# A unit's decay weights, issued four steps later in a hybrid SSD layer in fp32

## The chip, the cores and the metric

One core of one Trainium2 chip. The metric is the device time of one execution in microseconds (us), the median of several runs. Before the change it is 1293.44 us (three runs, 1293.35 to 1298.07).

## The reference

One layer of a trunk: RMSNorm, a Mamba-2 mixer (SSD) with residual, and a final RMSNorm, for 512 tokens of width 2048 in fp32. Cut to what matters here:

```python
proj = rmsnorm(x) @ w_in                     # 512 x 2048 @ 2048 x 10304: z, x, B, C, dt
xs, B, C = split(silu(conv4(proj_xbc)))      # causal depthwise convolution of 4 taps
dt = softplus(dt + dt_bias);  a = -exp(a_log) * dt
# scan over chunks, 64 heads of 64 in 8 groups, state 128:
cs = cumsum(a);  decay[l, s] = exp(cs[l] - cs[s]) for l >= s, else 0
y = (C.B * decay) @ (xs * dt) + C @ state * exp(cs)
y = (y + d_skip * xs) * silu(z)
out = rmsnorm(x + rmsnorm(y) @ w_out)
```

## The kernel before

**Two halves of a number.** TensorE multiplies in a rounded 32-bit format (fp32r). Each weight piece of 128x1024 therefore is split (`split_piece`): ScalarE makes `hi`, the rounded copy (L87), and VectorE `lo`, the rest (L88). A product is then three matmuls for each slice of the inner dimension: activations' `hi` and `lo` with weight `hi` (L635, L636), activations' `hi` with weight `lo` (L637).

**Pairs and products.** The columns of `w_in` are worked off in tiles of 128. The first eight tiles are multiplied plainly. The other 72 go two by two, in 36 *pairs* (`pair`), each by a scheme of seven half-size products in place of eight (Strassen's way, on the two tiles, the two halves of the inner dimension and the two halves of the tokens). A pair has 28 *steps*, four to a product. In TensorE's order: R11, T1, then the last product T4 of the pair before (`prev`), T2, R22, R21 and T3. T3 is the seventh product issued within a pair, at steps 24 to 27; its weights come from a raw buffer named `rb`, which SP fills with one piece (L81) and a DMA of GpSimd's queue adds another to (L598, `accum_op`). There is one `rb`; the next load into it waits for its `lo`.

**Units.** A pair of an x tile and a z tile is a *unit* of two heads, numbered 0 to 31. Of each group of four units, a pair of a B tile and a C tile (a *B/C pair*) comes ahead of the third. After its pair a unit is worked on in five functions, at steps counted from the start of its own pair: `u_load` (28: SP loads `csb` and `ecs`), `u_decay`, `u_xt` (56), `u_state` (65), `u_yd` (65), `u_yo` (71).

`u_decay` makes the decay weights `m`: twelve activations on ScalarE of 128x128 (L456, L457, L458), which read `csb`, an exponential over 128x1024 (L459), and on VectorE the product with the masked C·B (L461). `m` and `csb` have one buffer each. `u_yd` on TensorE (L502, L506) reads `m`. `u_yd`, `u_yo` and the convolution (`conv_silu`: L388, L391) follow on VectorE; `u_yo` ends with a store by SP (L524), behind which the next loads of SP stand.

**What sets the order.** The program is written through a table `ev` of steps: `add(step, f, ...)` puts a function in, and `product` calls `run(step)` before every second slice. TensorE, SP and GpSimd issue in the order in which the program is written. For ScalarE and VectorE a scheduler sets the order at build time, by what it thinks is ready; what is written earlier goes first, and what stands under `urgent()` ahead of that. T3's split is written at step 17 (`q_events`: `(17, q_split, ("T3",))`), T1's of the next pair at 18, R11's of the pair after it at 19.

**Kinds of pairs**, by which unit's decay they hold (it belongs to the pair ahead). In a cycle of five: the *B/C pair* holds that of units 5, 9, 13, 17, 21 and 25; the *gap pair* right after it holds none; the *restart pair* after that holds that of units 6, 10, 14, 18, 22 and 26; two *ordinary pairs* hold those of 7 and 8, 11 and 12, and so on. Unit 2's is held by the second of all pairs, units 3 and 4 and 27 to 30 are in ordinary pairs. The two first units have a table of their own (`ramp`).

Of the kernel before, what the change touches and what calls it, by code (L numbers as in the profile page):

```python
# [34 lines left out]
def mamba_layer(ctx: ExitStack, tc: tile.TileContext, d: dict, out: bass.AP):  # L35
# [668 lines left out]
    def add(step, f, *a):  # L704
        ev.setdefault(step, []).append((f, a))
# [4 lines left out]
            add(at["x", 4 * g] + 28, g_cb, g, i)  # L710
    ramp = [[66, 71, 63, 75, 87, 92], [56, 65, 50, 68, 86, 92]]
    for u in range(NU):
        w = ramp[u] if u < len(ramp) else [28, 42, 56, 65, 65, 71]
        for o, f in zip(w, (u_load, u_decay, u_xt, u_state, u_yd, u_yo)):
            add(at["x", u] + o, f, u)
    for n in range(len(quads)):
# [395 lines left out]
```

## Time and profile before

| | |
|---|---|
| median of three runs | 1293.44 us |
| the profiled execution | 1295.7 us |
| its span, first to last instruction | 1294.0 us |
| mean granted TensorE clock | 0.991 |
| TensorE busy | 1252.1 us (97%) |
| VectorE busy | 1084.3 us (84%) |
| ScalarE busy | 826.6 us (64%) |
| DMA moved | 225.90 MB, mean 175 GB/s |

In the profile PE is TensorE's matmul, PEld its weight load, DVE VectorE, ACT ScalarE, POOL GpSimd, and SPq the queue of SyncE, which issues DMAs. A timeline row has the start and the duration in us, engine, line, operation, tiles written <- read, form and count, and in brackets the engine's idle time just before it with what ended it. A row of waits names who waited for whom, the sum in us, how often, and the longest. A row of time slices has, after the span, the busy time of PE, PEld, DVE, ACT and POOL with their instructions, then the granted clock, the DMA engines' busy share and GB/s. Ends of matmuls are modelled and overlap; so where the text counts matmuls it goes by starts.

### The profile page before, as it was taken

To read this page: it belongs to the slowest core of one execution; us is meant where nothing else is said; L and a number is where in the kernel's file an instruction comes from. 1 tells how busy PE (TensorE), PEld (TensorE's weight loads), DVE (VectorE), ACT (ScalarE), POOL (GpSimd) and SP (SyncE) were. 2 spreads that over 40 slices of the span, in tenths; PEclk is the share of its full clock that TensorE was granted. 3 is DMA by queue.
4 is the path that set the end of the run, shared out by engine and by line. 5 is a ranking of instruction groups with operands and counts; after the bars stand their busy time and mean duration, and the time that the engine had idled before them with its cause. 6 is when DMAs were issued, how large, how long until landed. Compare 5 with 4: busy or idle time off the path is not lost.

```text
span 1294.0 us, 24519 instructions
## 1 busy us (share of the span) xinstructions
PE 1252.1 (97%) x9932; PEld 1192.9 (92%) x9932; DVE 1084.3 (84%) x1449; ACT 826.6 (64%) x1357; POOL 77.5 (6%) x99
## 2 busy tenths in 40 slices
PE   8989899999999999999999999999999899999997
PEld 8989899999999999999999999999988899899885
DVE  5796988988989898998889899889857877887865
ACT  7667667677666757767685867778666445434433
POOL 0000001010000101010100001000000000000000
PEclk9989999999999999999999999999999999999999
DMA  9546657585676667667667677766637576647612
GB/s 356 179 141 172 162 161 174 143 215 142 192 197 174 159 169 183 164 176 199 162 161 195 151 188 171 212 155 154 185 105 258 146 199 199 197 119 229 183 57 98
DMA packets 70194, 225.90 MB, mean 175 GB/s; under 512 B 8384, under 2 KB 12800, under 8 KB 69952
## 3 DMA queue, kind: packets, MB, share of 16 engines
q1 hardware_dynamic: 56688, 176.34, 40.2%
q0 software_dynamic: 12672, 46.14, 22.1%
q8 instruction: 78, 1.28, 0.4%
q10 hardware_dynamic: 720, 1.84, 0.4%
q14 instruction: 36, 0.29, 0.1%
HBM read 211.52 MB, written 12.78 MB: 173 GB/s over the span
## 4 chain that ended last, share of the span: by engine, by line
PE 74%; DVE 11%; DMA 7%; issue 4%; ACT 3%; SPq 0%; POOL 0%; DVEq 0%; ACTq 0%; POOLq 0%
PE S L637 7%; PE S L635 7%; PE S L636 7%; PE mm L635 5%; PE mm L636 4%; PE R L635 4%; PE mm L637 4%; PE R L636 4%; PE R L637 4%; DVE lo L88 3%; PE mm L929 3%; PE mm L931 3%; PE mm L930 3%; PE yd L502 2%; PE mm L867 2%
## 5 line engine op out<-in xcount | busy, mean ns | idle before, releaser
L87 ACT CAST hi<-ra 128x1024 fp32r<-128x1024 f32 x150 | 154.7, 1046 | 159.5 <-DVE ra L604 72.9
L88 DVE TENSOR_TENSOR lo<-ra,hi 128x1024 fp32r<-128x1024 f32 x150 | 181.3, 1221 | 24.2 <-ACT hi L87 24.1
L635 PE MATMUL mm<-xh,hi 128*128 128x256 f32 x576 | 163.6, 284 | 0.0
L637 PE MATMUL mm<-xh,lo 128*128 128x256 f32 x576 | 160.6, 279 | 0.6 <-DVE lo L88 0.6
L636 PE MATMUL mm<-xl,hi 128*128 128x256 f32 x576 | 160.4, 278 | 0.0
L637 PE MATMUL R<-s,lo 128*128 128x256 f32 x576 | 160.3, 278 | 0.1
L635 PE MATMUL R<-s,hi 128*128 128x256 f32 x576 | 160.2, 278 | 0.0
L636 PE MATMUL R<-s,hi 128*128 128x256 f32 x576 | 160.2, 278 | 0.0
L88 DVE TENSOR_TENSOR lo<-rc,hi 128x1024 fp32r<-128x1024 f32 x94 | 114.9, 1223 | 28.5 <-ACT hi L87 28.1
L87 ACT CAST hi<-rc 128x1024 fp32r<-128x1024 f32 x94 | 98.4, 1047 | 50.8 <-issue 29.1
L604 DVE TENSOR_TENSOR ra<-ra,rc 128x1024 f32<-128x1024 f32 x88 | 107.7, 1224 | 13.3 <-DMA rc<-in_wi 11.8
L635 PEld LDWEIGHTS mm<-xh,hi 128*128 128x128 f32 x576 | 108.1, 188 | 5.2 <-issue 5.0
L637 PEld LDWEIGHTS mm<-xh,lo 128*128 128x128 f32 x576 | 109.2, 190 | 0.8 <-DVE lo L88 0.8
L637 PEld LDWEIGHTS R<-s,lo 128*128 128x128 f32 x576 | 109.1, 189 | 0.3 <-DVE lo L88 0.3
L635 PEld LDWEIGHTS R<-s,hi 128*128 128x128 f32 x576 | 108.2, 188 | 0.0
L636 PEld LDWEIGHTS mm<-xl,hi 128*128 128x128 f32 x576 | 108.2, 188 | 0.0
L636 PEld LDWEIGHTS R<-s,hi 128*128 128x128 f32 x576 | 108.1, 188 | 0.0
L637 PE MATMUL S<-xh,lo 128*128 128x256 f32 x288 | 83.5, 290 | 5.6 <-DVE lo L88 5.6
L635 PE MATMUL S<-xh,h1h 128*128 128x256 f32 x288 | 83.4, 290 | 1.0 <-DVE xr L398 1.0
L635 PE MATMUL S<-xh,hi 128*128 128x256 f32 x288 | 81.3, 282 | 2.2 <-ACT xh L577 1.3
L636 PE MATMUL S<-xl,hi 128*128 128x256 f32 x288 | 81.2, 282 | 0.7 <-DVE xl L578 0.7
L636 PE MATMUL S<-xl,h1h 128*128 128x256 f32 x288 | 80.8, 280 | 0.0
(452 smaller groups left out, 3940.8 us busy)
## 6 DMA issues: line engine op xcount, KB each, us to landing
rc<-in_wi SPq DMA_DIRECT2D x76, 512.0 KB, 5.9
ra<-in_wi SPq DMA_DIRECT2D x42, 512.0 KB, 6.2
rb<-in_wi SPq DMA_DIRECT2D x40, 512.0 KB, 6.9
ra<-in_wi POOLq DMA_DIRECT2D x36, 512.0 KB, 6.3
rb<-in_wi POOLq DMA_DIRECT2D x36, 512.0 KB, 5.9
csb<-cscr SPq DMA_DIRECT2D x32, 512.0 KB, 8.0
ra<-in_wo SPq DMA_DIRECT2D x26, 512.0 KB, 5.4
yscr<-xs SPq DMA_DIRECT2D x32, 256.0 KB, 2.6
```

The lines of the kernel that those rows point to most:

```text
L87: S.copy(out=hi, in_=raw)
L88: V.tensor_tensor(out=lo, in0=raw, in1=hi, op=ALU.subtract)
L502: T.matmul(pyd[r, i, :], x[:, 2 * i, hh, :], m[:, i, hh::4, :], start=i == 0, stop=False, skip_group_check=True)
L604: V.tensor_tensor(out=raw, in0=raw, in1=qs[n][other], op=ALU.add)
L635: T.matmul(ps, hi[:, k, :], ah, start=first and k == 0, stop=False, skip_group_check=True)
L636: T.matmul(ps, hi[:, k, :], al, start=False, stop=False, skip_group_check=True)
L637: T.matmul(ps, lo[:, k, :], ah, start=False, stop=k == KH - 1, skip_group_check=True)
L867: T.matmul(ps[:, t, :], yh[:, k, tt], hi[:, k, :], start=st, stop=False, skip_group_check=True)
L929: T.matmul(ps, yh, hi, start=first and k == 0, stop=False)
L930: T.matmul(ps, yh, lo, start=False, stop=False)
L931: T.matmul(ps, yl, hi, start=False, stop=last and k == 1)
```

## The change

The second number of the table of a unit's steps: `u_decay` is written at step 46 after its pair's start in place of 42, which is step 18 of the pair that holds it in place of 14. It then stands behind T3's split (17) and, at the same step, ahead of T1's.

```diff
     for u in range(NU):
-        w = ramp[u] if u < len(ramp) else [28, 42, 56, 65, 65, 71]
+        w = ramp[u] if u < len(ramp) else [28, 46, 56, 65, 65, 71]
         for o, f in zip(w, (u_load, u_decay, u_xt, u_state, u_yd, u_yo)):
             add(at["x", u] + o, f, u)
```

The same instructions are issued as before. The order on TensorE, SP and GpSimd is the same row by row; on SP the load of `csb` now has a wait for ScalarE of its own in most units. On ScalarE and VectorE the order changes from unit 2 on.

First, ScalarE in the pair that holds unit 2's decay, from the copy out of PSUM (L674) on. L87 is the cast of T3's weights, L394 the silu of a convolution. Before:

```order
L674 COPY sn<-S 128x256
L458 ACTIVATE m<-csb,nwl 128x128
L456 ACTIVATE m<-csb,cs 128x128
L457 ACTIVATE m<-csb,cs 128x128
L458 ACTIVATE m<-csb,nwl 128x128
L456 ACTIVATE m<-csb,cs 128x128
L457 ACTIVATE m<-csb,cs 128x128
L458 ACTIVATE m<-csb,nwl 128x128
L459 ACTIVATE m<-m 128x2x512
L394 ACT_TABLE_LOAD
L394 ACTIVATE xs<-xs 128x512
L87 CAST hi<-rb 128x1024
```

After:

```order
L674 COPY sn<-S 128x256
L87 CAST hi<-rb 128x1024
L458 ACTIVATE m<-csb,nwl 128x128
L456 ACTIVATE m<-csb,cs 128x128
L457 ACTIVATE m<-csb,cs 128x128
```

The cast moved ahead of the last seven activations, the exponential and the silu. VectorE in the same pair, before and then after (L391: convolution, L679: half of z):

```order
L88 TENSOR_TENSOR lo<-rc,hi 128x1024
L391 SCALAR_TENSOR_TENSOR xs<-xr,par,xs 128x512 x2
L679 TENSOR_TENSOR z<-R,sn 128x256
L461 TENSOR_TENSOR m<-m,cbm 128x1536
L88 TENSOR_TENSOR lo<-rb,hi 128x1024
L88 TENSOR_TENSOR lo<-ra,hi 128x1024 x2
```

```order
L88 TENSOR_TENSOR lo<-rc,hi 128x1024
L391 SCALAR_TENSOR_TENSOR xs<-xr,par,xs 128x512
L88 TENSOR_TENSOR lo<-rb,hi 128x1024
L679 TENSOR_TENSOR z<-R,sn 128x256
L391 SCALAR_TENSOR_TENSOR xs<-xr,par,xs 128x512
L461 TENSOR_TENSOR m<-m,cbm 128x1536
L88 TENSOR_TENSOR lo<-ra,hi 128x1024 x2
```

T3's `lo` moved ahead of L461, of L679 and of one convolution step. VectorE in an ordinary pair (unit 3's decay; the others alike, and in B/C pairs L679 and `lo` both go ahead of L461), before and after:

```order
L523 TENSOR_TENSOR xs<-xs,z 128x512
L461 TENSOR_TENSOR m<-m,cbm 128x1536
L88 TENSOR_TENSOR lo<-rb,hi 128x1024
L529 TENSOR_TENSOR sx<-sx,z 128x512
L679 TENSOR_TENSOR z<-R,sn 128x256
```

```order
L523 TENSOR_TENSOR xs<-xs,z 128x512
L88 TENSOR_TENSOR lo<-rb,hi 128x1024
L461 TENSOR_TENSOR m<-m,cbm 128x1536
L529 TENSOR_TENSOR sx<-sx,z 128x512
L679 TENSOR_TENSOR z<-R,sn 128x256
```

L461 and T3's `lo` changed places; on ScalarE the cast of `rb` moved there ahead of the copy L674, the last L457 and L458, and L459. In the restart pairs the rows are the same before and after, on VectorE these (and on ScalarE the cast of `rb` behind L459):

```order
L391 SCALAR_TENSOR_TENSOR xs<-xr,par,xs 128x512 x2
L461 TENSOR_TENSOR m<-m,cbm 128x1536
L391 SCALAR_TENSOR_TENSOR xs<-xr,par,xs 128x512
L679 TENSOR_TENSOR z<-R,sn 128x256
L88 TENSOR_TENSOR lo<-rb,hi 128x1024
```

Nothing moved there.

## The prediction

> **What bounds the kernel now.** I read the page's head first, then TensorE's list of waits over the stretch in which the 36 pairs run (100 to 960 us), then the timelines at its waits.
>
> ```profile
> span 1294.0 us, 24519 instructions
> PE 1252.1 (97%) x9932; PEld 1192.9 (92%) x9932; DVE 1084.3 (84%) x1449; ACT 826.6 (64%) x1357; POOL 77.5 (6%) x99
> PE S L637 <- DVE lo L88: 5.6, 9, 1.5
> ```
>
> TensorE is busy for 97%, so only its waits can be gained. The largest group among the pairs is `S L637 <- lo`: 5.6 us in nine places. All nine lie in the seventh product (T3), whose rounded weights `hi` and rest `lo` are made from the buffer `rb`. These are the rows of five of those pairs, and of one whose wait is too small for the list.
>
> ```profile
> 163.27 0.28 PE L637 MATMUL mm<-xh,lo 128*128 128x256 f32 x1
> 164.45 0.38 PE L635 MATMUL S<-xh,hi 128*128 128x256 f32 x1 [0.91 <-ACT hi L87]
> 165.71 0.58 PE L637 MATMUL S<-xh,lo 128*128 128x256 f32 x1 [0.76 <-DVE lo L88]
> 235.69 0.28 PE L636 MATMUL S<-xl,hi 128*128 128x256 f32 x1
> 236.13 0.39 PE L637 MATMUL S<-xh,lo 128*128 128x256 f32 x1 [0.17 <-DVE lo L88]
> 347.12 0.39 PE L637 MATMUL S<-xh,lo 128*128 128x256 f32 x1 [0.17 <-DVE lo L88]
> 390.02 0.38 PE L637 MATMUL S<-xh,lo 128*128 128x256 f32 x1 [0.47 <-DVE lo L88]
> 501.43 0.39 PE L637 MATMUL S<-xh,lo 128*128 128x256 f32 x1 [1.54 <-DVE lo L88]
> 412.39 0.38 PE L637 MATMUL S<-xh,lo 128*128 128x256 f32 x1
> 412.60 0.28 PE L635 MATMUL S<-xh,hi 128*128 128x256 f32 x1
> ```
>
> Matmuls normally start 0.11 to 0.12 us apart. A wait costs more than its idle time: 235.69 to 236.13 is 0.44, so 0.33 too long, and the start after the first `lo` matmul comes 0.10 late, as 412.39 to 412.60 shows. So the small waits (0.17) cost about 0.42 us each, and a pair whose `lo` comes just in time (412) costs 0.10.
>
> The pairs fall in kinds (named in the kernel section). Unit 2 waits at 164; restart pairs have the big waits (0.47 at 390, 1.54 at 501; of the 5.6 us they hold four, about 4.2); B/C pairs have 0.17 each (236 and 347 are two); ordinary pairs have the 0.10.
>
> **Unit 2, the pair at 164 us.** ScalarE casts T3's `hi` after the whole decay and a silu, and VectorE subtracts after the product with the masked C·B (L461).
>
> ```profile
> 158.14 0.37 ACT L674 COPY sn<-S 128x256 f32<-128x256 f32 x1
> 158.41 0.41 ACT L458 ACTIVATE m<-csb,nwl 128x128 f32<-128x128 f32 x1
> 163.37 1.03 ACT L87 CAST hi<-rb 128x1024 fp32r<-128x1024 f32 x1
> 159.60 1.53 DVE L391 SCALAR_TENSOR_TENSOR xs<-xr,par,xs 128x512 f32<-128x512 f32 x2
> 161.55 1.76 DVE L461 TENSOR_TENSOR m<-m,cbm 128x1536 f32<-128x1536 f32 x1
> 164.43 1.23 DVE L88 TENSOR_TENSOR lo<-rb,hi 128x1024 fp32r<-128x1024 f32 x1 [1.12 <-ACT hi L87]
> 141.70 0.88 POOL L598 DMA_DIRECT2D rb<-in_wi  x1 [9.09 <-DVE xr L576]
> rb<-in_wi POOLq DMA_DIRECT2D x36, 512.0 KB, 5.9
> 165.57 2.35 DVE L88 TENSOR_TENSOR lo<-ra,hi 128x1024 fp32r<-128x1024 f32 x2
> 177.03 0.65 PE L502 MATMUL yd<-m,xd 128*64 128x256 f32 x4
> 158.89:162.30 3.41, 3.41 (x33) 3.41 (x32) 3.29 (x5) 3.39 (x8) 0.00 (x0) 1.00 1.02 315
> 162.30:165.71 3.41, 1.74 (x13) 1.34 (x12) 2.29 (x3) 3.40 (x5) 0.00 (x0) 1.00 0.48 183
> 165.71:169.12 3.41, 3.41 (x16) 3.41 (x17) 3.35 (x3) 0.58 (x1) 0.00 (x0) 0.50 0.66 193
> ```
>
> In the new order the cast follows the copy at 158.14, so it can run 158.41 to 159.4; `rb` was asked for at 141.70 and at the median landing time of 5.9 us was there by 147.6. VectorE's first of the two convolution steps ends about 160.3, then `lo` takes 1.1 to 1.2 (from start to next start), until about 161.5. T3 could start at 163.27 + 0.11 = 163.4, so both waits go. What they cost: 1.18 + 1.04 us between starts where 0.11 each is normal, plus 0.4 in the two ramps after them, 2.4 us. The three slices at the end of the fence tell the rest; the third number from the right is TensorE's granted clock. After the slice with the waits (13 matmuls) it is 0.50 for one slice (16 matmuls); undisturbed, a slice holds 33. 29 matmuls are 29/33 x 3.41 = 3.0 us of work, done in 6.8: 3.8 us, of which I take 3.7. So the half clock is 1.3 of it. What is put behind has cover: ScalarE's decay ends 1.0 later, at 162.5, L461 follows until about 164.2, and the first reader of `m` stands at 177.03, some 9 us later when all moves up by 3.7. Next late would be the second product's `lo<-ra`, the first of the two that run from 165.57: it is ready at 166.8 as before, and TensorE would now want it at 163.4 + 2.7 (T3) + 0.4 (transposes) + 2.8 (first product) = 169.3.
>
> [...]
>
> **Ordinary and B/C pairs.**
>
> ```profile
> 407.77 1.05 ACT L459 ACTIVATE m<-m 128x1024 f32<-128x1024 f32 x1
> 408.73 1.04 ACT L87 CAST hi<-rb 128x1024 fp32r<-128x1024 f32 x1
> 409.44 1.75 DVE L461 TENSOR_TENSOR m<-m,cbm 128x1536 f32<-128x1536 f32 x1
> 411.11 1.22 DVE L88 TENSOR_TENSOR lo<-rb,hi 128x1024 fp32r<-128x1024 f32 x1
> 423.42 0.44 PE L502 MATMUL yd<-m,xd 128*64 128x256 f32 x2
> 338.27 0.69 DVE L398 TENSOR_TENSOR xr<-mm,rbc 128x512 f32<-128x512 f32 x1 [1.50 <-PE mm L637]
> 338.27:367.77 29.50, 29.33 (x257) 28.56 (x256) 29.46 (x42) 19.50 (x34) 1.73 (x2) 1.00 0.59 146
> ```
>
> The cast moves ahead of the last two decay steps and the exponential over all of `m`, some 1.8 us; `lo` and L461 change places, so `lo` ends at 410.7 where it ended at 412.3. L461 then starts at 410.6; its input, ready at 408.8, comes 1.0 later, 409.8, so nothing waits. It ends at 412.3, 11 us ahead of `yd` (423.42). SP's next load of `rb` waits for this `lo` (one buffer), so it and the csb load behind it go out about 1.7 us earlier; csb must now wait for the decay's last read, about 408.8, ahead of that. On POOL's queue the accumulate into `rb` comes earlier too. DMA is the same in kind and amount.
>
> The waits that stay won: unit 5's B/C pair (236), 0.42, since its restart pair has no wait now; the 0.10 of row 412.60, in ten ordinary pairs of units 7 to 30, 1.0. Together 1.4.
>
> The B/C pairs' waits are not won for good. From the convolution at 338.27, the last place where VectorE waited for TensorE, to `lo` at 367.77 it is busy for 29.46 of 29.50 us: its time is then set by its own work, which the swap leaves as it was. What hangs on its end is the restart pair:
>
> ```profile
> 368.63 0.62 SPq L440 DMA_DIRECT2D csb<-cscr  x1
> 377.53 0.40 ACT L456 ACTIVATE m<-csb,cs 128x128 f32<-128x128 f32 x1 [0.39 <-DMA csb<-cscr]
> 388.75 1.22 DVE L88 TENSOR_TENSOR lo<-rb,hi 128x1024 fp32r<-128x1024 f32 x1
> ```
>
> SP issues csb right after that `lo`, it lands 8.9 us later, ScalarE starts the decay at once, and T3's `lo` follows at 388.75. In the restart pairs the rows of VectorE and ScalarE stand in the old order (last extract of the change): L461 is still ahead of `lo`. A TensorE that is 0.42 earlier out of the B/C pair waits 0.42 longer here. So for units 9, 21, 25 (0.42) and 13, 17 (0.10) I count nothing, and nothing for the 4.2 us of the restart pairs.
>
> **Sum:** 3.7 + 1.4 = 5.1 us. The profiled execution took 1295.7, 1.7 outside its span of 1294.0; it becomes 1290.6. It lies 2.3 above the median of 1293.44, from which the forecast is 1288.3, 0.40% less. Runs of this kernel tell 0.5% (6.5 us) from no change, so this is within it.
>
> One thing is not in the sum: the matmul pace.
>
> ```profile
> 241.93:244.65 2.72, 2.72 (x27) 2.72 (x26) 2.72 (x5) 1.32 (x2) 0.84 (x1) 1.00 0.07 27
> 264.03:266.85 2.82, 2.82 (x26) 2.82 (x25) 2.79 (x3) 2.81 (x6) 0.86 (x1) 1.00 0.53 114
> ```
>
> These are two second products of 24 equal matmuls, no wait in either: 2.72 and 2.82 us. Which pace holds changes only where the stream is broken (a wait, the small matmuls of a unit), and every removed wait may change what follows. Over 36 x 7 = 252 products that is 25 us between all slow and all fast; some 70 independent stretches, split evenly, give about ±2 us (an estimate from these rows). It takes no side.
>
> **Rivals.**
> 1. More than 0.5% faster: the pace falls on the fast side by 2 us, or csb lands 0.5 us earlier in the five restart pairs because `rb` and csb of the pairs ahead are out of the way sooner (2.5 us). Either gives about 1286, both 1283.8. For it: csb took 8.9 us here, with four weight loads ahead of it. Against: those four stand as before.
> 2. Unit 2 gives less. (a) The half clock does not hang on these waits and stays: 1.3 less, 1289.6; against it, the slice of 0.50 follows the waits at once. [...] (b) Another wait takes the place at 164 us: up to 3.7 less, 1292.0; against it, the 2.5 us that `lo<-ra` has to spare.
> 3. The swap frees nothing: all waits reappear in the restart pairs, 1293.4. Against: between unit 2 and the next restart pair VectorE waits for TensorE at L398, as at 338.27, and so moves up with it.
> 4. Slower: the cast, now earlier in ScalarE's order, waits for `rb`, and everything behind it waits too.
>
> ```profile
> 333.36 0.87 POOL L598 DMA_DIRECT2D rb<-in_wi  x1 [20.59 <-DMA rb<-in_wi]
> 343.12 1.03 ACT L87 CAST hi<-rb 128x1024 fp32r<-128x1024 f32 x1
> ```
>
> At unit 9 it moves from 343.1 to 341.3 us; issued at 333.4, `rb` has 2 us to spare at 5.9. TensorE, which reads this `lo` from about 346.8, feels a landing only after 344.2, that is from 10.8 us on; at 11.1 us, 0.3 in each of some 24 pairs, it costs 7 us, 1300. The median is half of that.
>
> **Chances:** the forecast 0.52 (its own range 1286 to 1290.8, a quarter of it beyond 0.5%), rival 1 0.22, rival 2 0.17 (a 0.09, b 0.08), rival 3 0.05, rival 4 0.04. Range 1284.5 to 1292.5, which leaves out the slower case, no gain at all, and the far end of rival 1. Faster by over 0.5%: 0.22 + 0.13 = 0.35; slower 0.04; the rest 0.61.
>
> **What would show it.** No wait and no clock of 0.50 near 160 to 170 us; `lo<-rb` ahead of L461 by a clear margin, and no `S L637 <- lo` wait in ordinary and B/C pairs; four or five such waits left, all in restart pairs, the ones after B/C pairs longer by up to 0.4. If the restart pairs' waits vanish too, my chain from csb is wrong; if unit 2's time does not come back, rival 2.

## The result, and the profile after

| | before | after |
|---|---|---|
| median | 1293.35 us, 7 runs (1289.91 to 1298.07) | 1285.82 us, 7 runs (1283.94 to 1287.64) |
| profiled execution | 1295.7 us | 1284.84 us |
| its span | 1294.0 us | 1283.1 us |

The ratio is 0.9934, 95% interval 0.9916 to 0.9951: 0.66% less, 6 to 11 us. The forecast was 1288.3, so the gain is inside the range given and 2.5 us larger than forecast. The time is that of rival 1, by its pace half.

The head of the page after, and TensorE's largest wait among the pairs:

```profile
span 1283.1 us, 24537 instructions
PE 1242.2 (97%) x9932; PEld 1183.7 (92%) x9932; DVE 1084.2 (84%) x1449; ACT 829.1 (65%) x1357; POOL 77.7 (6%) x99
PE S L637 <- DVE lo L88: 7.5, 6, 1.8
```

The wait for T3's `lo` fell from nine places to six, but grew from 5.6 to 7.5 us: all six are restart pairs. TensorE's busy time fell by 9.9 us though it does the same matmuls (the 18 instructions more are waits for semaphores, 14 of them SP's ahead of `csb`). Most of that, 6.9 us by the count below, is the pace, the part that the forecast left at nothing.

**Unit 2.** TensorE's timeline at its T3, then ScalarE's and VectorE's around it, and two slices of 3.41 us from T3 on, with the clock, which was 0.50 behind this place before:

```profile
161.61 0.28 PE L637 MATMUL mm<-xh,lo 128*128 128x256 f32 x1
161.73 0.28 PE L635 MATMUL S<-xh,hi 128*128 128x256 f32 x1
161.96 0.28 PE L637 MATMUL S<-xh,lo 128*128 128x256 f32 x1
156.54 1.06 ACT L87 CAST hi<-rb 128x1024 fp32r<-128x1024 f32 x1
158.07 1.22 DVE L88 TENSOR_TENSOR lo<-rb,hi 128x1024 fp32r<-128x1024 f32 x1
160.65 1.76 DVE L461 TENSOR_TENSOR m<-m,cbm 128x1536 f32<-128x1536 f32 x1 [0.37 <-ACT m L459]
161.47:164.88 3.41, 3.41 (x31) 3.41 (x30) 2.28 (x3) 2.98 (x4) 0.73 (x1) 1.00 0.93 371
164.88:168.29 3.41, 3.41 (x32) 3.41 (x31) 3.41 (x6) 1.18 (x3) 0.13 (x1) 1.00 0.75 91
```

`lo` ends at 159.29, 2.4 us ahead of T3; no wait, and the clock stays at 1.00.

**Restart pairs.** The two whose waits were 0.47 (at 390) and 1.54 (at 501) before:

```profile
382.21 0.39 PE L637 MATMUL S<-xh,lo 128*128 128x256 f32 x1 [1.56 <-DVE lo L88]
493.66 0.39 PE L637 MATMUL S<-xh,lo 128*128 128x256 f32 x1 [1.83 <-DVE lo L88]
491.60:495.00 3.40, 1.57 (x14) 1.37 (x13) 3.37 (x5) 2.78 (x3) 0.00 (x0) 1.00 0.29 107
495.00:498.40 3.40, 3.40 (x18) 3.40 (x17) 2.56 (x3) 0.93 (x1) 0.37 (x1) 0.50 0.95 321
```

Both waits grew. After the slice that holds the second (14 matmuls) the clock is 0.50 for one slice: the half clock that went at 165 us came back at 495. Matmuls start 0.21 us apart in that slice in place of 0.11, which over its 3.40 us comes to about 1.6 us.

**An ordinary pair** (unit 7), TensorE around T3's first `lo` matmul, before and then after:

```profile
300.32 0.28 PE L637 MATMUL mm<-xh,lo 128*128 128x256 f32 x1
300.66 0.39 PE L637 MATMUL S<-xh,lo 128*128 128x256 f32 x1
300.88 0.28 PE L635 MATMUL S<-xh,hi 128*128 128x256 f32 x1
301.00 0.28 PE L636 MATMUL S<-xl,hi 128*128 128x256 f32 x1
297.71:300.43 2.72, 2.72 (x26) 2.72 (x25) 2.72 (x3) 2.69 (x5) 0.00 (x0) 1.00 0.63 193
307.93:310.75 2.82, 2.82 (x26) 2.82 (x25) 2.79 (x4) 1.64 (x3) 0.86 (x1) 1.00 0.36 80
```

```profile
293.45 0.28 PE L637 MATMUL mm<-xh,lo 128*128 128x256 f32 x1
293.79 0.28 PE L637 MATMUL S<-xh,lo 128*128 128x256 f32 x1
293.90 0.28 PE L635 MATMUL S<-xh,hi 128*128 128x256 f32 x1
290.84:293.56 2.72, 2.72 (x26) 2.72 (x25) 2.72 (x3) 2.69 (x4) 0.00 (x0) 1.00 0.65 182
300.76:303.48 2.72, 2.72 (x26) 2.72 (x25) 2.69 (x5) 1.85 (x3) 0.86 (x1) 1.00 0.30 100
```

Before, the start behind the first `lo` matmul comes 0.22 after it in place of 0.11. It cost 0.10 there, as the forecast had it. But the product ahead of this T3 took 2.72 us and the second product behind it 2.82: the small lateness was where the slow pace began. After, with `lo` 1.5 us ahead, the pace stays at 2.72.

Counted over the trace (starts of neighbouring matmuls of the pairs 112 to 114 ns apart are fast, 117 to 119 slow): 3018 fast and 2766 slow before, 4575 and 1222 after. The means are 113.34 and 117.78 ns. 1557 more starts at the shorter distance, by 4.44 ns each, are 6.9 us. *Fast share* below is the part that fast starts have in both kinds together.

**Where the 10.9 us between the two spans went**, read from the start of T3's first `lo` matmul in each unit's pair: 2.25 us lie ahead of unit 2 (a half clock at 77 us lasted two slices in one execution and one in the other, in code that the change leaves alone); 3.5 are unit 2's; 4.3 lie between units 3 and 30; 0.85 in the tail. The medians lie only 7.5 apart; the 2.25 and the 0.85, 3.1 in all, lie ahead of the first pair that the change touches and behind the last.

### The profile page after: what moved, and what is told of

The parts are those of the page before. It is cut to its first block, busy times and chain, and to the rows that moved or that the text cites. A ratio compares the mean times of both kernels' runs of the same rounds, so it can differ in the third digit from the quotient of the medians.

```text
span 1283.1 us, 24537 instructions
## 1 busy us (share of the span) xinstructions
PE 1242.2 (97%) x9932; PEld 1183.7 (92%) x9932; DVE 1084.2 (84%) x1449; ACT 829.1 (65%) x1357; POOL 77.7 (6%) x99
## 3 DMA queue, kind: packets, MB, share of 16 engines
q10 hardware_dynamic: 720, 1.84, 0.4%
## 4 chain that ended last, share of the span: by engine, by line
PE 72%; DVE 12%; DMA 8%; issue 4%; ACT 3%; SPq 0%; POOL 0%; DVEq 0%; ACTq 0%; POOLq 0%
PE S L637 6%; PE S L635 6%; PE S L636 6%; PE mm L635 4%; PE R L635 4%; PE R L637 4%; PE R L636 4%; PE mm L636 4%; PE mm L637 4%; DVE lo L88 3%; PE mm L929 3%; PE mm L931 3%; PE mm L930 3%; PE mm L867 3%; PE mm L868 3%
## 5 line engine op out<-in xcount | busy, mean ns | idle before, releaser
L87 ACT CAST hi<-ra 128x1024 fp32r<-128x1024 f32 x150 | 155.2, 1049 | 152.2 <-DVE ra L604 86.1
L88 DVE TENSOR_TENSOR lo<-rc,hi 128x1024 fp32r<-128x1024 f32 x94 | 114.9, 1222 | 23.6 <-ACT hi L87 23.3
L87 ACT CAST hi<-rc 128x1024 fp32r<-128x1024 f32 x94 | 98.7, 1050 | 44.7 <-issue 22.8
L604 DVE TENSOR_TENSOR ra<-ra,rc 128x1024 f32<-128x1024 f32 x88 | 107.7, 1224 | 13.3 <-DMA rc<-in_wi 11.9
```

The source lines that it names most:

```text
L87: S.copy(out=hi, in_=raw)
L88: V.tensor_tensor(out=lo, in0=raw, in1=hi, op=ALU.subtract)
L604: V.tensor_tensor(out=raw, in0=raw, in1=qs[n][other], op=ALU.add)
```

## The experiments

Theory W says that only waits and their ramps count, and that the pace falls by chance; theory P that a late `lo` at T3 starts a slow stretch. The kernel before was timed again with each set of runs (medians 1293.71, 1293.87 and 1294.92 us); a ratio is to the one of its own set.

**Only unit 2.**

```diff
- [28, 42, 56, 65, 65, 71]
+ [28, 46 if u == 2 else 42, 56, 65, 65, 71]
```

> Step 46 for unit 2 alone, 42 for all others. Both theories expect what the prediction counted for unit 2: 3.7 us off the kernel before (ratio 0.997), no slice at half clock near 165 us, T3's lo ready about 2 us early in that pair. The theory that only waits count (W) and the theory that T3's late lo also sets the matmul pace (P) agree here: the share of matmuls that start 112 to 114 ns apart stays near the 52% of before, since the other units keep the late lo.

Measured 1290.22 us, ratio 0.9970 (0.9954 to 0.9986): 3.9 us by the ratio, 3.5 by the medians, against 3.7 forecast. Fast share 54%. No slice of 0.50 lies near 165 us. Unit 2's term stands.

**All but unit 2** (`42 if u == 2 else 46`).

> Step 46 for every unit but 2. Theory W: 1.4 us off the kernel before (ratio 0.9989), the pace as it falls, near 52% fast. Theory P: a late lo, even by 0.1 us, breaks the stream and leaves the next stretch at the slow pace; with lo ready the fast pace holds through ordinary pairs, so the fast share is 75% or more, as in the changed kernel (79%), and 4 to 5 us go (ratio 0.996 to 0.997). Unit 2's waits and the half clock near 165 us stay under both.

Measured 1290.81 us, ratio 0.9978 (0.9963 to 0.9994), 2.8 us. Fast share 80%. The wait and the half clock at 165 us stay, and in one restart pair the clock drops as in the changed kernel (first two rows); behind a wait as long, at 499.57, it does not (next two):

```profile
383.60:387.00 3.40, 1.56 (x14) 1.37 (x13) 3.40 (x5) 3.37 (x4) 0.00 (x0) 0.99 0.56 213
387.00:390.40 3.40, 3.40 (x18) 3.40 (x17) 3.14 (x3) 0.39 (x1) 0.00 (x0) 0.50 0.73 231
496.20:499.61 3.41, 1.57 (x15) 1.37 (x13) 3.41 (x5) 3.38 (x5) 0.00 (x0) 1.00 0.58 205
499.61:503.00 3.39, 3.39 (x30) 3.39 (x31) 3.36 (x4) 1.34 (x2) 0.00 (x0) 1.00 0.64 203
PE S L637 <- DVE lo L88: 8.9, 7, 1.8
```

So the pace does go over to the fast side. The time alone does not decide: its interval holds both W's 0.9989 and P's 0.996 to 0.997. The restart pairs, which hold 8.2 of the 8.9 us, take part of the pace back.

**The split earlier instead of the decay later**: T3's split written at step 13, the decay left at 42.

```diff
- (17, q_split, ("T3",))
+ (13, q_split, ("T3",))
```

> The decay back at step 42, and in its place T3's split issued four steps earlier (13 in place of 17), so that it is ahead of the decay from the other side. In this order T3's lo goes ahead of L461 in the restart pairs too, and ScalarE has six table loads more per cycle or fewer. If the lateness of T3's lo is all that counts: at least what the changed kernel gained (7.5 us), and the restart pairs' waits (7.5 us in six) shrink below 2 us in all, together 1277 to 1283. If the decay's later place itself counts (csb's load, SP's queue, ScalarE's order): no better than the kernel before, 1290 to 1294, with new waits elsewhere.

Measured 1308.65 us, ratio 1.0115 (1.0091 to 1.0139): slower than either expectation. TensorE waits elsewhere, on ScalarE's copies (L684) and on the `lo` of other products; that the scheduler moved this work behind the earlier cast is an inference from its rule and was not followed row by row:

```profile
PE mm L635 <- ACT mm L684: 6.3, 5, 1.8
PE S L637 <- DVE lo L88: 4.7, 9, 1.2
PE R L637 <- DVE lo L88: 4.1, 5, 1.0
PE S L929 <- ACT hi L87: 3.3, 1, 3.3
```

It is another order and not the same change from the other side; on W and P its time says nothing.

**The ordinary pairs alone, and the B/C pairs alone**, each with unit 2.

```diff
+ [28, 46 if u == 2 or u % UPG in (0, 3) else 42, 56, 65, 65, 71]   # ordinary (not units 29 and 30)
+ [28, 46 if u == 2 or u % UPG == 1 else 42, 56, 65, 65, 71]        # B/C (and unit 29)
```

> Decay at step 46 for unit 2 and for the units in ordinary pairs (3, 4, 7, 8, 11, 12 and so on); at 42, as before, for the units in B/C and restart pairs. Theory P (a `lo` that is late at T3, by however little, puts TensorE back on the slow matmul pace for the products behind it): the ordinary pairs' share of the pace comes with it. Fast starts rise from 52% to about 68%, slow ones fall to about 1850, worth some 4 us beside the 3.7 of unit 2 and the 1.0 of the ordinary pairs' own lateness: 1285 to 1286.5. Theory W (only the waits count, and the pace falls by chance): 3.7 + 1.0, 1289.0, with a fast share that need not move. In both the restart pairs' waits stay near those of before (5 us in 8 places), since the B/C pairs are as before.

> The other half: decay at step 46 for unit 2 and for the units in B/C pairs (5, 9, 13, 17, 21, 25), at 42 for all others. Theory P: the B/C pair's late `lo` goes, so the products of the gap pair behind it run fast; fast share about 62%, 2 to 2.5 us beside the 3.7 of unit 2 and 0.4 of unit 5, given back in part by longer waits in the restart pairs (6 to 7.5 us in all): 1287.5 to 1288.5. Theory W: 3.7 + 0.4, and the B/C pairs' own 0.42 handed on to the restart pairs: 1289.5.

Measured: ordinary 1286.43 us, ratio 0.9927 (0.9903 to 0.9950), fast share 64%; B/C 1290.30 us, ratio 0.9963 (0.9946 to 0.9979), fast share 52%. The ordinary half gives what the change gives beside unit 2, 3.8 us by the medians where their own lateness is 1.0. That is outside W (1289.0, a ratio of 0.9962) and within P's 1285 to 1286.5. The B/C half adds nothing that shows to unit 2. Its interval holds both W's 1289.5 and P's 1287.5 to 1288.5, but the fast share that P forecast, about 62%, did not come. The gap pairs stayed slow although no T3 of a B/C pair has a late `lo` any more: in all six the slow stretch (240 to 249 starts) begins within T4, behind the small matmuls of a unit (L488, L502, L506). Two equal products of the gap pair at 350 us, ahead of these matmuls and behind them:

```profile
349.71:352.43 2.72, 2.72 (x26) 2.72 (x25) 2.72 (x6) 1.37 (x3) 0.86 (x1) 1.00 0.09 11
360.50:363.32 2.82, 2.82 (x26) 2.82 (x25) 2.82 (x7) 1.43 (x3) 0.00 (x0) 1.00 0.02 6
```

**`csb` earlier in the restart pairs** (16, 20 or 6 in place of 28, on the changed kernel). The edit takes in units 2 and 30 too, which also leave 2 on division by four.

```diff
- [28, 46, 56, 65, 65, 71]
+ [16 if u % UPG == 2 else 28, 46, 56, 65, 65, 71]   # 20 and 6 in the others
```

> The changed kernel, with the csb and ecs loads of the restart pairs' units written 12 steps earlier (16 in place of 28), ahead of the four weight loads in SP's order; VectorE still has L461 ahead of T3's lo there. Theory C (restart waits hang on csb's landing): csb lands about 4 us earlier in those pairs, the six waits of 1.2 to 2 us go or fall below 0.5, and 5 to 7 us go on top of the changed kernel, about 1279 to 1281. Theory V (they hang on VectorE's own work from the B/C pair on): the waits stay within 0.5 us of what they are and the time is the changed kernel's, 1285 to 1287.

> The changed kernel, with the loads of `csb` and `ecs` for the restart pairs' units at step 20 in place of 28. There the scheduler puts T3's `lo` ahead of the last convolution step and of L679 (some 1.0 to 1.1 us of VectorE), but still behind L461. Theory V (VectorE's own row of work sets when `lo` comes in a restart pair): `lo` comes 1.0 to 1.5 us earlier than in the changed kernel, the waits there fall from 7.5 to about 1 us, the half clock after 491 us goes: about 1279. Theory C (the landing of `csb` sets it, through the decay on ScalarE): with `csb` asked for earlier the waits go too; what tells the two apart is the room ahead of `lo` on VectorE. By V VectorE is busy without a break from the convolution to `lo`; by C it stands idle ahead of L461.

> The changed kernel, with those loads at step 6: the decay of the restart pairs' units then runs one pair earlier, in the gap pair, and L461 no longer stands ahead of T3's `lo` in the restart pair, which so comes some 2 us earlier there. V and C alike: no wait for `lo` in the restart pairs, 7.5 us less, with the half clock after 491 us gone some 8: 1278 to 1279. Against it: twelve more loads of an activation table on ScalarE in the gap pairs and L461 among VectorE's work there, which could make T3's or the next product's split late in the gap pair; each wait of 0.5 us there would cost 3 us over six pairs, 1281. Pace: with only the B/C pairs' stretch left slow, the fast share stays near 80% or rises.

Step 16: 1283.35 us, ratio 0.9913 (0.9887 to 0.9939); one of its six runs took 3897.62 us and is not in the ratio, the others took 1281.09 to 1284.54. Step 20: 1284.74, ratio 0.9919 (0.9897 to 0.9940). Step 6: 1275.67, ratio 0.9857 (0.9833 to 0.9881). The waits for T3's `lo`, in this order (with step 6 none is left):

```profile
PE S L637 <- DVE lo L88: 5.9, 6, 1.5
PE S L637 <- DVE lo L88: 3.0, 5, 0.7
```

With steps 16 and 20 neither theory's forecast came: the waits shrank from 7.5 us, but five of six stayed above the 0.5 us of C (step 16), and all together above V's 1 us (step 20), and the times lie outside C's 1279 to 1281 and V's 1285 to 1287 (step 16) and V's 1279 (step 20).

ScalarE and VectorE in one restart pair (unit 10), in the changed kernel and then with step 16:

```profile
364.15 1.23 DVE L604 TENSOR_TENSOR ra<-ra,rc 128x1024 f32<-128x1024 f32 x1 [2.05 <-DMA rc<-in_wi]
369.71 0.41 ACT L456 ACTIVATE m<-csb,cs 128x128 f32<-128x128 f32 x1 [0.25 <-DMA csb<-cscr]
376.85 1.04 ACT L459 ACTIVATE m<-m 128x1024 f32<-128x1024 f32 x1
378.05 1.06 ACT L87 CAST hi<-rb 128x1024 fp32r<-128x1024 f32 x1
378.28 1.75 DVE L461 TENSOR_TENSOR m<-m,cbm 128x1536 f32<-128x1536 f32 x1
380.94 1.22 DVE L88 TENSOR_TENSOR lo<-rb,hi 128x1024 fp32r<-128x1024 f32 x1
```

```profile
366.12 0.40 ACT L456 ACTIVATE m<-csb,cs 128x128 f32<-128x128 f32 x1 [0.77 <-DMA csb<-cscr]
370.00 1.23 DVE L604 TENSOR_TENSOR ra<-ra,rc 128x1024 f32<-128x1024 f32 x1 [2.50 <-DMA rc<-in_wi]
380.54 1.04 ACT L459 ACTIVATE m<-m 128x1024 f32<-128x1024 f32 x1
384.41 1.22 DVE L88 TENSOR_TENSOR lo<-rb,hi 128x1024 fp32r<-128x1024 f32 x1
```

With step 16 TensorE stands 2.93 us later here, from the gap pair to the fifth product of this pair. Taken off, the decay began 6.5 us earlier, yet its exponential began 0.8 later (380.54 less 2.93 against 376.85) and `lo` 0.5 later. TensorE itself came 0.65 later still to T3, so the wait is 0.1 shorter (1.45 against 1.56). Theory C alone is wrong, then: with `csb` out of the way something else holds the decay. The row that moved is the landing of `rc`: L604, which waits for it, now starts 2.9 us later (370.00 less 2.93 against 364.15), and casts on ScalarE follow from it. Nor is V right in its strict form, since VectorE stands idle for 2.50 us on the way. What holds T3's `lo` back is that the decay's twelve activations, its exponential and L461 stand in this pair ahead of it: with step 6 they are done in the gap pair, and the wait goes.

**What the change is worth where nothing is taken back**: `csb` at step 6 in all three; all decays at 42; at 46 but in B/C pairs; at 46 again.

```diff
+ [6 if u % UPG == 2 else 28, 42, 56, 65, 65, 71]
+ [6 if u % UPG == 2 else 28, 46 if u == 2 or u % UPG in (0, 2, 3) else 42, 56, 65, 65, 71]   # 42: B/C and unit 29
+ [6 if u % UPG == 2 else 28, 46, 56, 65, 65, 71]
```

> The kernel before, with the loads of `csb` and `ecs` for the restart pairs' units at step 6, so without a wait for `lo` in a restart pair, and with every decay still at 42. Against the same kernel with the decays at 46 (1275.67 us) this shows what the change is worth where the restart pairs can take nothing back. Theory G (what the B/C pairs win, in waits and in pace, is taken back in the restart pairs of the changed kernel): unit 2's 3.7, ten ordinary pairs' 1.0, six B/C pairs' 0.42 = 2.5, and the whole of the pace, some 6.9: 14 in all, 1289 to 1290, with a fast share near 50%. Rival W (pace by chance): 7.2, 1283. Rival N (the step in B/C pairs is worth nothing in itself): 3.7 + 1.0 + 2.8, 1283.

> The version with `csb` and `ecs` at step 6 and the decays at 46, with one thing undone: the units in B/C pairs (5, 9, 13, 17, 21, 25) at 42. Theory G (their gain is real and was only taken back in the restart pairs): 6 x 0.42 = 2.5 us of waits come back, and slow pace for some six products behind each, 6 x 6 x 24 matmuls x 4.45 ns = 3.8: 1279.5 to 1282 where the version itself took 1275.67; fast share some 15 points lower than in it. Theory N (nothing is lost with it): 1275 to 1277.

> The version with `csb` and `ecs` at step 6 and all decays at 46 once more, beside the two above. Its profiled execution was the slowest of its six (1281.7, where the others took 1273.5 to 1279.1). Theory P: an execution of 1274 to 1276 shows a fast share of 85% or more, against 76% in the one of 1281.7, with the same waits: 1370 slow starts less 300 to 900 would be 1.3 to 4 us. Rival: the difference lies in the start (the time of the first tiles) or in half-clock slices, and the fast share is the same. Median 1274 to 1278 again.

Measured, in this order: 1288.26 us, ratio 0.9950 (0.9934 to 0.9967), fast share 49%; 1279.00, 0.9886 (0.9867 to 0.9905), 68%; 1278.12, 0.9873 (0.9856 to 0.9890), 79%. One thing in these forecasts is wrong: they count unit 2's 3.7 us, but `csb` at step 6 takes in unit 2 and takes its wait away already with the decay at 42. TensorE's first `lo` matmul of T3 there:

```profile
162.90 0.28 PE L637 MATMUL S<-xh,lo 128*128 128x256 f32 x1
```

No slice of 0.50 lies near it either. So the change is worth 10.1 us by the medians here, with nothing from unit 2. Without the earlier `csb` it was worth 7.5, of which 3.7 are unit 2's. Less the 3.7, theory G expects 10.4, W 3.5 and N 3.8: G's sum is met. The slow starts fall from 2946 to 1219, which at 4.44 ns is 7.7 us: where no restart pair waits, the pace arrives in full. That B/C pairs are worth something by themselves stays open: 0.9 us between the medians, with intervals that overlap. One thing that takes from them is seen in the last kernel, a wait behind ScalarE that the second lacks:

```profile
PE tr L473 <- ACT xs L394: 1.4, 3, 0.8
```

What was expected of the repeat stays untested, since no execution of 1274 to 1276 was profiled: the one profiled took 1279.77 and shows a fast share of 79% against 76% in the one of 1281.7. The one of 1281.7 had a slice of half clock at 715 us and 3.3 us of that wait for L394, so the rival there is the nearer one.

**Pace and lateness over all kernels.** `lo` of T3 late by 0.1 us or more in some or all of the pairs named, restart pairs apart, and the share of fast starts counted as above (the kernel with the split at step 13 is left out of the table):

| late in | kernels | fast share |
|---|---|---|
| ordinary and B/C pairs | before; only unit 2; `csb` 6, decay 42 | 52, 54, 49% |
| ordinary pairs | B/C alone | 52% |
| B/C pairs | ordinary alone; `csb` 6, B/C at 42 | 64, 68% |
| neither (unit 2 aside) | after; all but unit 2; `csb` 16, 20, 6, 6 | 79, 80, 81, 75, 76, 79% |

Where the ordinary pairs are late the share is 49 to 54%, whether the B/C pairs are late or not; where the B/C pairs are late and the ordinary ones are not, 64 and 68%; where neither is, 75% or more. So the pace follows the lateness, that of the ordinary pairs above all, and does not fall by chance alone. The kernel with the split at step 13 does not fit in: there `lo` comes 0.23 to 0.79 us late in five of these pairs, and its fast share is 72%.

Where the slow stretches begin says how far the cause is shown. Before, from unit 3's pair on, seven begin at T3 of an ordinary pair, right behind a late `lo` (162 to 183 slow starts each, 1256 together). In the eight kernels of the table whose ordinary pairs are in time (in one of them all but the last pair), no such stretch of more than 20 starts begins there. That half of theory P is shown, except that L461 always changes its place together with the lateness, so that its place is not told apart from it. Five more begin within T4, in four gap pairs and in unit 3's pair, behind a unit's small matmuls (257 to 278 each, 1344 together). After the change both kinds are gone, and seven shorter ones (110 each) begin within T4 of the B/C pairs and of one ordinary pair, with no `lo` late, beside two of 49 and 73 in restart pairs. What decides the pace at the small matmuls stays open; a late `lo` just ahead is not needed.

## Why the prediction was right or wrong

- **Unit 2, 3.7 us: right.** 3.5 between the traces; with unit 2 alone 3.9 by the ratio (1.8 to 6.0) and 3.5 by the medians. T3 had room as worked out, and the half clock went with the waits; rival 2 is out.
- **The half clock behind a wait: not behind every wait of that length.** In the changed kernel the clock was 0.50 for a slice behind the wait of 1.83 us at 493.66 (TensorE busy for 1.57 of the 3.40 us from 491.60), and 1.00 behind the one of 1.56 us at 382.21. With all but unit 2 changed, TensorE was busy for 1.56 of 3.40 us from 383.60 and for 1.57 of 3.41 from 496.20; the clock was 0.50 behind the first and 1.00 behind the second.
- **No wait in ordinary and B/C pairs: right.** `lo` stands 1.50 us ahead of T3 in the first (1.18 in the last pair of all) and 1.83 in the second. The swap with L461 on VectorE cost nothing: in these pairs `yd` still comes 9.2 us or more behind L461's end.
- **The B/C pairs' gain given back: right, and larger than forecast.** "Up to 0.4" longer was expected of four or five waits; six came, and 390's grew by 1.1. What is given back is the pace above all. Four restart pairs stood behind a slow gap pair before (257 to 278 slow starts, 1.1 to 1.2 us); after, TensorE comes 0.8 to 1.1 us earlier to their `lo`, which does not move with it. In the other two, whose gap pair was fast already, the wait went from 1.54 to 1.83 and from 1.33 to 0.96. **Unit 5's 0.42, counted as won for good, was not:** its restart pair, without a wait before, now waits 0.63 us at 271.51. The reason named, VectorE's own work from 338 to 367, is only part. Of the chain that the prediction drew from the landing of `csb`, the runs with steps 16 and 20 show that an earlier first link shortens the waits from 7.5 only to 5.9 and 3.0 us; taking the decay out of the pair (step 6) ends them.
- **"It takes no side": this step failed.** The pace was seen, its two values and where it changes were read rightly, and its size of 25 us between all slow and all fast as well. But it was treated as a coin over some 70 independent stretches. They are not independent: pairs of one kind mostly fall alike. In before's own rows ten ordinary pairs' T3 had a late `lo`, and in seven of them slow matmuls start right behind it; the term of those pairs was then not ten times 0.10 but the slow stretches too. 1.0 became some 3.8 (the run with the ordinary pairs alone).
- **What the terms left at nothing came to.** The pace in all brought 6.9 us, of which the growth of the restart waits (some 3.3, from about 4.2 to 7.5) and the half clock at 495 (1.6) took most back again. With the other waits gone (1.0, unit 5's 0.42 and some 1.5 in the other B/C pairs) that is about 4.9; 4.3 was seen between units 3 and 30, where 1.4 was forecast. That the time stayed so near the forecast is luck in part: 6.9 us won and 4.9 lost, neither of them in the sum, cancelled for the most part.
- **Rival 1: its time came, by its first half.** `csb` was not what brought it: it still took 8.6 us in the changed kernel (issued at 361.1, waited for until 369.7). **Rivals 3 and 4** did not come about; no cast of `rb` waited for its landing in an ordinary or B/C pair.

## What to carry to other kernels

Here a late operand cost more than its wait: in seven ordinary pairs a `lo` that made the next start come 0.10 us late was followed by 162 to 183 starts 117.8 ns apart in place of 113.3, another 0.7 to 0.8 us each. So compare the time of equal products on both sides of each small wait before calling it 0.1 us. What was won upstream came back in part as longer waits in a stage held by its own work (about 4.2 us in the restart pairs became 7.5), and behind one of these, of 1.83 us, the clock was 0.50 for a slice of 3.40 us; look for what fills that stage. Here the change alone gave 0.9934 and moving the decay out of the restart pairs alone (`csb` at step 6, decay at 42) 0.9950; the two together gave 0.9857 and 0.9873, more than the sum, though both take the same 3.7 us of unit 2 (the two figures are of two sets of runs). Writing one thing later and another earlier are not two ways to the same order when a scheduler fills the engines: here the second cost 1.2%.

## What was not expected of the hardware

In the traces before and after, equal matmuls of 128x256 mostly start 112 to 114 or 117 to 119 ns apart (means 113.3 and 117.8), and within a row of starts 110 to 121 ns apart no change from one pace to the other was found. Each half clock among the pairs (at 145 and 165 us before, at 143 and 495 after) lasted 3.41 us. A wait of 1.83 us (in the slice from 491.60) was followed by it and one of 1.56 us at 382.21 was not; with all but unit 2 changed, of two slices with the same 1.84 us of idle (from 383.60 and from 496.20) only one was, so what decides stays open. A product of 24 matmuls took 2.82 us in place of 2.72 at the slower pace, and the half clock at 495 cost about 1.6 us, beside waits of 0.17 to 1.83 us. Neither is seen in a list of waits.
